# Experts on one Trainium2 core: a second pair of PSUM banks for gate and up, gathers that skip empty slots, and a first gather ahead of the gates

## The chip, the cores and the metric

The kernel runs on one core of one Trainium2 chip. The metric is the device time of one execution in microseconds (us), the median of several runs. The engines of the core are PE (TensorE: matmuls and transposes; its weight loads are listed apart as PEld), DVE (VectorE), ACT (ScalarE), POOL (GpSimd) and SP (SyncE, which only starts transfers). Matmul results land in PSUM, which has eight banks of 128 x 512 float32; all that an engine multiplies or adds lies in SBUF, and weights come from the chip's memory by DMA.

## The reference

Two transformer blocks are computed for 512 tokens of width 1024. The change is in the second block's last layer, a mixture of 32 experts in 4 groups of 8: each token takes the best group, and in it the best two experts. The final norm follows it.

```python
def hier_moe(hn, w_rg, b_rg, w_re, b_re, w_gate, w_up, w_down):
    g_prob = jax.nn.softmax((xt @ w_rg + b_rg).astype(jnp.float32), axis=-1)
    p_grp, grp = lax.top_k(g_prob, 1)
    e_logits = (xt @ w_re + b_re).astype(jnp.float32).reshape(T, N_GROUPS, EXPERTS_PER_GROUP)
    e_logits = jnp.take_along_axis(e_logits, grp[:, :, None], axis=1)[:, 0]
    p_e, e_loc = lax.top_k(jax.nn.softmax(e_logits, axis=-1), TOP_K_INNER)
    gate = p_grp * p_e / jnp.sum(p_e, -1, keepdims=True)
    expert = grp * EXPERTS_PER_GROUP + e_loc
    ...
    def run_block(args):                 # the tokens of one expert
        e, toks, gts = args
        xb = x_pad[toks]
        hid = jax.nn.silu(xb @ w_gate[e]) * (xb @ w_up[e])
        return (hid @ w_down[e]) * gts[:, None].astype(xb.dtype)
    ...                                  # added back to the tokens' rows
```

The width of an expert's hidden layer is 512. 512 tokens with two experts each are 1024 assignments.

## The kernel before

The first 1,700 us or so are the first block and the attention and projections of the second; the change doesn't touch them. What follows is the router and the experts.

**Router** (class `Router`). For each of the four blocks of 128 tokens, `block` works out the logits, the two chosen experts, and `R[token, expert]`: the token's place in the expert's queue, counted from 1, or 0 where the token isn't of that expert (L1858). `full` (L1861) finds experts with more tokens than the 64 places that each has (CAP, L1701); `gates` (L1871) makes the gate weights `Gt`.

**Slots** (L1937). The experts are taken in pairs: pair n is experts 2n and 2n+1, whose 64 places each make 128 slots on the 128 partitions. `gather(n)` (L1950) makes four 0/1 matrices OH (token by slot, L1954, DVE), multiplies them by the table `ti` of 68 columns (token number, gates and norm factors, each in two parts; L1959, four matmuls, which need the gates), reads the token number of each slot (L1961, L1964) and has POOL fetch the 128 rows of 4 KB from memory by an indirect DMA (L1966). A slot that no token holds gets row 0. The rest of the table gives the slot's scale factors (L1970 to L1975). `turned(xs)` (L1978) turns the fetched rows with two times four transposes on PE (L1985) and copies them out of PSUM (one of the two copies by ACT, one by DVE, L174 and L178).

**moe** (L1990). The loop goes over q = 0 to 7 and pr = 0, 1; n = 2q + pr. For each n:
- CT, the transposed 0/1 matrix, by DVE (L2000).
- gate into PSUM bank G and up into bank U (L2001, both of the name "f", which has two banks): 64 matmuls of 64 columns by 512 (L2008), with the weights of the two experts in the two halves of PE's columns.
- silu(G) * U into `hid` (`silu_mul`, ACT L1894, DVE L1895 and L1896), four transposes of `hid` (L2014), a copy (hT).
- down: 2 x 16 matmuls (L2024) into a bank of the name "s"; ACT and DVE take it out as yhi (L2027) and ylo (L2028).
- `turned` for n+1 and `gather` for n+2.
- After every second n (and after n = 14) the results are added to the tokens' rows: for each of 2 halves of the columns and 4 token blocks one **scatter** group, four matmuls (two after n = 14; L1934) of CT with yhi and ylo into a bank, and one DVE addition x += bank (L2045). The banks of the four blocks are "pv", "acc", "s", "s" (L2043).

PSUM's eight banks are "f" x2, "s" x2, "tp" x2 (all transposes, and gather's table), "pv" x1, "acc" x1. A name's banks are handed out in turn (`acc`, L145), and the next holder waits until the last reader of the one before is done.

**Weights** (class `Experts`, L1900). 192 pieces of 1 MB, each fetched by two transfers of 512 KB from SP's queue (one piece by POOL's) into 16 buffers in turn (L1919), in the order in which moe uses them.

**Tail** (L2048 to L2075). The last pair's scatter, the final norm's sums of squares (ACT), two `rsqrt` for two token blocks each, scaling of both halves of the columns (ACT h0, DVE h1), and eight transfers out.

`moe_rest` (L2078) handles experts with more than 64 tokens; PE and the other engines load its count `ni` and jump past it (L2086, L2087), since there are none.

The order of the instructions on an engine isn't that of the source: the program is laid out by a planner that places each instruction where it expects it to be ready. The trace shows the order that came out (scatter groups stand between the down matmuls and the next gate matmuls, for instance).

Of the kernel before, what the change touches and what calls it, by code (L numbers as in the profile page):

```python
# [11 lines left out]
F32 = mybir.dt.float32  # L12
F32R = mybir.dt.float32r
# [1923 lines left out]
class Slots:  # L1937


    def __init__(self, K, keep, xnd, Gt, R, r4, pool, mc):  # L1940
        self.K, self.xnd, self.R, self.pool, self.mc = K, xnd, R, pool, mc
        nc = K.nc
        self.ti = ti = keep.tile([P, 4, 68], F32R, name="ti")
        nc.vector.tensor_copy(ti[:, :, 0:2], mc["tok2"].rearrange("p (b c) -> p b c", b=4))
        K.split(ti[:, :, 2:34], ti[:, :, 34:66], Gt)
        K.split(ti[:, :, 66:67], ti[:, :, 67:68], r4[:, :, None])
        self.ready = [self.gather(0), self.gather(1)]

    def gather(self, n):
        K, nc, pool = self.K, self.K.nc, self.pool  # L1950
        e0 = 2 * n
        OH = pool.tile([P, 4, P], F32R, name="OH", bufs=2)
        for b in range(4):
            nc.vector.tensor_tensor(OH[:, b].rearrange("p (e s) -> p e s", e=2),  # L1954
                                    self.mc["iota64"][:, None, :].to_broadcast([P, 2, 64]),
                                    self.R[:, b, e0:e0 + 2, None].to_broadcast([P, 2, 64]), op=OP.is_equal)
        pt = K.acc("tp")
        for b in range(4):
            nc.tensor.matmul(pt[:, :68], OH[:, b], self.ti[:, b], start=b == 0, stop=b == 3)  # L1959
        tg = K.sm.tile([P, 4], F32, name="tg")  # L1960
        nc.vector.tensor_copy(tg[:, 0:1], pt[:, 0:1])  # L1961

        row = K.sm.tile([P, 1], I32, name="row")
        nc.vector.tensor_scalar(row, pt[:, 0:1], -1.0, 0.0, op0=OP.add, op1=OP.max)  # L1964
        xs = pool.tile([P, D], F32, name="xs", bufs=2)
        nc.gpsimd.indirect_dma_start(xs, None, self.xnd, bass.IndirectOffsetOnAxis(ap=row[:, 0:1], axis=0))  # L1966
        for s in range(2):
            hs = slice(64 * s, 64 * s + 64)
            e = e0 + s
            nc.vector.tensor_copy(tg[hs, 1:2], pt[hs, 2 + e:3 + e])  # L1970
            nc.vector.tensor_add(tg[hs, 1:2], tg[hs, 1:2], pt[hs, 34 + e:35 + e])
        nc.vector.tensor_copy(tg[:, 2:3], pt[:, 66:67])
        nc.vector.tensor_add(tg[:, 2:3], tg[:, 2:3], pt[:, 67:68])
# [422 lines left out]
```

## Time and profile before

| | us |
|---|---|
| median of 3 runs | 2228.69 (2226.29 to 2232.9) |
| the profiled execution, its own time | 2238.75 |
| its span, first to last instruction | 2237.0 |
| mean granted TensorE clock in it | 0.965 |
| from the first expert's gate matmul (1727.61) to the last down matmuls' begin (2214.36) | 486.75 |
| one q in the middle of it (four experts) | 62.56 |

All times of single instructions below are positions in the span of the profiled execution, which took 10.06 us more than the median of the runs. A row of a timeline gives the start, the duration, the engine, the line of the kernel, what is written and read, how many instructions stand together, and in brackets an idle time of the engine before it and what ended that.

### The profile page before, as it was taken

What the parts mean: (1) busy time and instruction counts of PE and PEld (TensorE: products, weight loads), DVE (VectorE), ACT (ScalarE), POOL (GpSimd) and SP (SyncE); (2) the same over time, 40 slices, a digit from 0 to 9 for tenths busy, and PEclk for the clock granted to TensorE, in tenths of its full rate; (3) what the DMA queues carried; (4) which work ended last, traced back from release to release, by engine and by line L of the source; (5) the groups of instructions that cost most, each with busy time, mean ns of one, the idle gap of its engine ahead of it and who ended that gap; (6) DMA issues with size and microseconds to landing.
All of it is one profiled execution on the core that took longest, in us unless ns stands there. A gap on an engine that the chain in (4) does not pass through costs nothing.

```text
span 2237.0 us, 28592 instructions
## 1 busy us (share of the span) xinstructions
PE 2086.9 (93%) x10252; PEld 1476.5 (66%) x10252; DVE 1074.4 (48%) x2554; ACT 712.5 (32%) x1507; POOL 485.6 (22%) x391
## 2 busy tenths in 40 slices
PE   7999899998999999979988999999997999999997
PEld 5777676686888888867777867777875433333332
DVE  5272226427764545475877656555445322222223
ACT  4253334433353434234532235543441110000102
POOL 2312331233133222233331121232131000000000
PEclk9899999999999999999998799999998999999999
DMA  5512332256242332133334342485257999999994
GB/s 174 162 47 67 94 97 73 67 173 230 73 138 96 98 99 95 58 112 107 101 116 108 105 162 91 156 260 167 94 187 264 403 416 413 413 415 414 413 415 182
DMA packets 203370, 411.39 MB, mean 184 GB/s; under 512 B 49192, under 2 KB 67752, under 8 KB 203096
## 3 DMA queue, kind: packets, MB, share of 16 engines
q1 hardware_dynamic: 200632, 400.08, 51.0%
q0 software_dynamic: 2592, 9.44, 1.1%
q8 instruction: 82, 1.34, 0.3%
q14 instruction: 64, 0.52, 0.1%
HBM read 371.46 MB, written 33.13 MB: 181 GB/s over the span
## 4 chain that ended last, share of the span: by engine, by line
PE 68%; DVE 12%; DMA 7%; issue 3%; ACT 3%; POOL 2%; SPq 0%; DVEq 0%; ACTq 0%; POOLq 0%
PE f L135 23%; PE f L2008 10%; PE s L2024 6%; PE acc L135 6%; PE s L135 6%; PE tp L135 2%; POOL w L128 2%; PE pv L269 1%; PE tp L261 1%; PE s L1934 1%; DMA wraw<-w2f 1%; PE pv L135 1%; ACT w L125 1%; DMA wraw<-wout 1%; PE pv L1934 1%
## 5 line engine op out<-in xcount | busy, mean ns | idle before, releaser
L128 POOL TENSOR_TENSOR w<-wraw,w 128x512 fp32r<-128x512 f32 x310 | 407.2, 1325 | 1074.1 <-ACT w L125 962.0
L125 ACT CAST w<-wraw 128x512 fp32r<-128x512 f32 (+1 forms) x446 | 261.6, 617 | 242.2 <-issue 51.7
L135 PE MATMUL f<-hhi,w 128*128 128x512 f32 (+1 forms) x832 | 281.0, 410 | 2.0 <-ACT w L125 0.7
L128 DVE TENSOR_TENSOR w<-wraw,w 128x512 fp32r<-128x512 f32 (+1 forms) x136 | 116.3, 856 | 189.6 <-ACT w L125 186.5
L2008 PE MATMUL f<-mw,xT 128*64 128x512 f32 x832 | 206.8, 594 | 0.0
L135 PE MATMUL f<-h2hi,w 128*128 128x512 f32 (+1 forms) x672 | 203.7, 384 | 0.3 <-POOL w L128 0.3
L135 PEld LDWEIGHTS f<-hhi,w 128*128 128x128 f32 x832 | 161.8, 200 | 35.1 <-issue 3.2
L135 PE MATMUL acc<-hhi,w 128*128 128x512 f32 (+1 forms) x512 | 169.3, 398 | 4.9 <-ACT w L125 1.9
L135 PE MATMUL f<-hlo,w 128*128 128x512 f32 (+1 forms) x416 | 170.0, 409 | 0.2 <-DVE hlo L187 0.2
L2008 PEld LDWEIGHTS f<-mw,xT 128*64 128x64 f32 x832 | 65.5, 137 | 124.6 <-issue 117.7
L135 PEld LDWEIGHTS f<-h2hi,w 128*128 128x128 f32 x672 | 125.2, 188 | 25.6 <-POOL w L128 0.5
L135 PE MATMUL f<-h2lo,w 128*128 128x512 f32 (+1 forms) x336 | 129.0, 384 | 0.0
L2024 PE MATMUL s<-mw,hT 128*64 128x512 f32 x416 | 121.8, 600 | 3.3 <-ACT hT L174 1.9
L135 PEld LDWEIGHTS acc<-hhi,w 128*128 128x128 f32 x512 | 96.3, 191 | 28.5 <-issue 4.3
L1966 POOL DMA_INDIRECT xs<-xnd,row x16 | 15.2, 953 | 423.3 <-DVE wraw L2000 171.0
L135 PE MATMUL acc<-hlo,w 128*128 128x512 f32 (+1 forms) x256 | 101.3, 396 | 0.0
L135 PEld LDWEIGHTS f<-hlo,w 128*128 128x128 f32 x416 | 83.1, 200 | 16.2 <-issue 1.4
L1895 DVE SCALAR_TENSOR_TENSOR hid<-hid,f 128x512 f32<-128x512 f32 x16 | 11.0, 688 | 160.3 <-ACT hid L1894 160.3
L1894 ACT ACTIVATE hid<-f,tg 128x512 f32<-128x512 f32 x16 | 11.0, 688 | 204.1 <-PE f L2008 204.1
L2024 PEld LDWEIGHTS s<-mw,hT 128*64 128x64 f32 x416 | 33.2, 136 | 59.6 <-issue 51.5
L135 PEld LDWEIGHTS f<-h2lo,w 128*128 128x128 f32 x336 | 63.1, 188 | 12.3
L2027 ACT ACTIVATE yhi<-s,tg 128x512 fp32r<-128x512 f32 x32 | 22.0, 688 | 150.8 <-PE s L2024 150.8
(743 smaller groups left out, 3991.4 us busy)
## 6 DMA issues: line engine op xcount, KB each, us to landing
mw<-wexp SPq DMA_DIRECT2D x310, 512.0 KB
w<-wexp SPq DMA_DIRECT2D x72, 512.0 KB
wraw<-wup SPq DMA_DIRECT2D x88, 256.0 KB
wraw<-w2f SPq DMA_DIRECT2D x76, 256.0 KB
wraw<-wgate SPq DMA_DIRECT2D x64, 256.0 KB
wraw<-wdown SPq DMA_DIRECT2D x44, 256.0 KB
wraw<-w1f SPq DMA_DIRECT2D x40, 256.0 KB
gated<-gt SPq DMA_DIRECT2D x28, 256.0 KB
```

What stands on the lines that cost most here:

```text
L125: nc.scalar.copy(hi[:, s], raw)
L128: eng.tensor_sub(lo[:, s], raw, hi[:, s].bitcast(F32))
L135: self.nc.tensor.matmul(out, l, r, start=start and i == 0, stop=stop and i == 2)
L261: nc.tensor.transpose(pt[:, off:off + P], Pt[s][i][:, j * P:(j + 1) * P], K.ident)
L269: one = lambda s: nc.tensor.matmul(o[64 * s:64 * s + 64, j * P:], v_of(j, s), ptS[s][:, at[j]:at[j] + n], start=start and j == 0, stop=sto ...
L1894: nc.scalar.activation(t, G, AF.Tanh, scale=half)
L1895: nc.vector.scalar_tensor_tensor(t, t, 1.0, G, op0=OP.add, op1=OP.mult)
L1934: K.nc.tensor.matmul(o, CT[:, b * P:(b + 1) * P], y[:, hs], start=start and i == 0, stop=i == len(items) - 1)
L1966: nc.gpsimd.indirect_dma_start(xs, None, self.xnd, bass.IndirectOffsetOnAxis(ap=row[:, 0:1], axis=0))
L2008: nc.tensor.matmul(o[64 * s:64 * s + 64], xT[:, kk, 64 * s:64 * s + 64], ws[s][k], start=kk == 0, stop=kk == 7)
L2024: nc.tensor.matmul(o[64 * s:64 * s + 64], hT[:, c, 64 * s:64 * s + 64], ws[s][c], start=c == 0, stop=c == 3)
L2027: nc.scalar.activation(yhi[:, hs], o, AF.Copy, scale=tg[:, 1:2])
```

## The change

- `Slots` is made early, in front of the router, with its tiles in the pool `keep`; its table is split into `tok` (2 columns) and `ti` (66 columns). Two of its row buffers are set to zero by POOL.
- `gather` becomes `rows` and `scales`. `rows(n)` makes OH, multiplies it by `tok` alone, and asks for the rows. A slot without a token gets a row number above 511, and the transfer leaves such rows out (bounds_check). `scales(n)` multiplies OH by the rest of the table in four further matmuls.
- `first()` asks for the rows of pairs 0 and 1 before the gates are computed; `router.full` comes after.
- G and U are the two "f" banks for pr = 0, and "pv" and "acc" for pr = 1.
- All scatter groups use the two "s" banks, which down uses too.
- The tail makes one `rsqrt` for all four token blocks, and scales and sends the second half of the columns first; the first half is scaled by ACT and POOL in turn.

```diff
 class Slots:
-        self.ti = ti = keep.tile([P, 4, 68], F32R, name="ti")
...
-        self.ready = [self.gather(0), self.gather(1)]
+        self.tok = keep.tile([P, 4, 2], F32R, name="tok")
+        nc.vector.tensor_copy(self.tok, mc["tok2"].rearrange("p (b c) -> p b c", b=4))
+        self.ti = keep.tile([P, 4, 66], F32R, name="ti")
+        self.xs = [keep.tile([P, D], F32, name="xs", bufs=2) for _ in range(2)]
+        for t in self.xs:
+            nc.gpsimd.memset(t, 0.0)
+    def first(self, R, Gt, r4):
+        self.R = R
+        rows = [self.rows(n) for n in range(2)]
+        K, ti = self.K, self.ti
+        K.split(ti[:, :, 0:32], ti[:, :, 32:64], Gt())
+        K.split(ti[:, :, 64:65], ti[:, :, 65:66], r4[:, :, None])
+        self.ready = [self.scales(*r) for r in rows]
     def gather(self, n):
+        return self.scales(*self.rows(n))
+    def rows(self, n):
...
         for b in range(4):
-            nc.tensor.matmul(pt[:, :68], OH[:, b], self.ti[:, b], start=b == 0, stop=b == 3)
+            nc.tensor.matmul(pt[:, :2], OH[:, b], self.tok[:, b], start=b == 0, stop=b == 3)
...
+        none = K.sm.tile([P, 1], F32, name="none")
+        nc.vector.tensor_scalar(none, pt[:, 0:1], 0.5, 2.0 * T, op0=OP.is_lt, op1=OP.mult)
+        row = K.sm.tile([P, 1], I32, name="row")
+        nc.vector.scalar_tensor_tensor(row, pt[:, 0:1], -1.0, none, op0=OP.add, op1=OP.add)
         nc.vector.tensor_copy(tg[:, 0:1], pt[:, 0:1])
-        row = K.sm.tile([P, 1], I32, name="row")
-        nc.vector.tensor_scalar(row, pt[:, 0:1], -1.0, 0.0, op0=OP.add, op1=OP.max)
-        xs = pool.tile([P, D], F32, name="xs", bufs=2)
-        nc.gpsimd.indirect_dma_start(xs, None, self.xnd, bass.IndirectOffsetOnAxis(ap=row[:, 0:1], axis=0))
+        xs = self.xs[n] if n < 2 else pool.tile([P, D], F32, name="xs", bufs=2)
+        nc.gpsimd.indirect_dma_start(xs, None, self.xnd, bass.IndirectOffsetOnAxis(ap=row[:, 0:1], axis=0),
+                                     bounds_check=T - 1, oob_is_err=False)
+        return n, OH, tg, xs
+    def scales(self, n, OH, tg, xs):
+        pt = K.acc("tp")
+        for b in range(4):
+            nc.tensor.matmul(pt[:, :66], OH[:, b], self.ti[:, b], start=b == 0, stop=b == 3)
...
 def moe(K, x, slots, weights, pool, mc, out):
-            G, U = K.acc("f"), K.acc("f")
+            G, U = (K.acc(t) for t in (("f", "f"), ("pv", "acc"))[pr])
...
-                    o = K.acc(("pv", "acc", "s", "s")[b])
+                    o = K.acc("s")
...
-    os_ = [K.acc(t) for t in ("pv", "acc", "f", "f")]
+    os_ = [K.acc(t) for t in ("f", "f", "pv", "acc")]
...
-    for p in range(2):
-        for b in (2 * p, 2 * p + 1):
-            nc.scalar.activation(j[:, h1], os_[b], AF.Square, accum_out=ss[:, b, 1:2])
-        s = ss[:, 2 * p:2 * p + 2]
-        nc.vector.tensor_add(s[:, :, 0], s[:, :, 0], s[:, :, 1])
-        r = K.rsqrt(s[:, :, 0], 1.0 / D, 1e-6, 2)
...
+    for b in range(4):
+        nc.scalar.activation(j[:, h1], os_[b], AF.Square, accum_out=ss[:, b, 1:2])
+    nc.vector.tensor_add(ss[:, :, 0], ss[:, :, 0], ss[:, :, 1])
+    r = K.rsqrt(ss[:, :, 0], 1.0 / D, 1e-6, 4)
+    for b in range(4):
+        rows = out[b * P:(b + 1) * P]
+        nc.vector.scalar_tensor_tensor(x[:, b, h1], os_[b], r[:, b:b + 1], g[:, h1], op0=OP.mult, op1=OP.mult)
+        nc.sync.dma_start(rows[:, h1], x[:, b, h1])
+        if b % 2:
+            nc.gpsimd.tensor_scalar(x[:, b, h0], x[:, b, h0], r[:, b:b + 1], None, op0=OP.mult)
+        else:
+            nc.scalar.activation(x[:, b, h0], x[:, b, h0], AF.Copy, scale=r[:, b:b + 1])
+        nc.sync.dma_start(rows[:, h0], x[:, b, h0])
...
-    upto, ni = router.full(keep)
-    Gt = router.gates(keep)
+    g = []
+    slots.first(router.R, lambda: g.append(router.gates(keep)) or g[0], r4)
+    Gt = g[0]
+    upto, ni = router.full(keep)
     RT.close()
...
-    slots = Slots(K, keep, xnd, Gt, router.R, r4, K.pool(E, "slots"), mc)
```

## Rows read from the trace of the kernel before

**Rows 1.** The page's first part: busy time, share of span, count of instructions.

```profile
PE 2086.9 (93%) x10252; PEld 1476.5 (66%) x10252; DVE 1074.4 (48%) x2554; ACT 712.5 (32%) x1507; POOL 485.6 (22%) x391
```

**Rows 2.** Windows: one q's length, five engines' busy times, clock, DMA share, GB/s.

```profile
1845.62:1908.18 62.56, 60.18 (x258) 23.46 (x260) 17.45 (x50) 5.88 (x9) 1.88 (x2) 1.00 1.03 413
```

**Rows 3.** PE's waits by releaser, 1750 to 2190: sum, count, median of one.

```profile
PE tp L2014 <- DVE hid L1896: 11.0, 13, 0.9
PE s L2024 <- DVE hT L178: 2.4, 7, 0.3
PE s L2024 <- ACT hT L174: 1.9, 7, 0.3
```

**Rows 4.** The same for SP's queue, which starts the weights' transfers.

```profile
SPq L1919 <- DMA mw<-wexp: 259.2, 272, 2.8
SPq L1919 <- PE f L2008: 3.7, 14, 0.5
```

**Rows 5.** Instruction groups by form, 1740 to 2190: busy, mean ns, idle before.

```profile
L2008 PE MATMUL f<-mw,xT 128*64 128x512 f32 x746 | 184.7, 593 | 0.0
```

**Rows 6.** Timeline of PE, pair 1: the gather's four matmuls and what follows.

```profile
1776.94 0.61 PE L1959 MATMUL tp<-ti,OH 128*128 128x68 f32 x4
1777.39 0.48 PE L1934 MATMUL pv<-yhi,wraw 128*128 128x512 f32 x1
```

**Rows 7.** Timeline of PE, pairs 6 to 8: gate, down and scatter matmuls.

```profile
1908.11 13.95 PE L2008 MATMUL f<-mw,xT 128*64 128x512 f32 x62
...
1929.99 1.07 PE L2024 MATMUL s<-w,hT 128*64 128x512 f32 x2
1930.99 0.50 PE L1934 MATMUL pv<-yhi,wraw 128*128 128x512 f32 x1
...
1958.98 0.40 PE L1934 MATMUL pv<-ylo,wraw 128*128 128x512 f32 x1
...
1960.16 0.40 PE L1934 MATMUL s<-ylo,wraw 128*128 128x512 f32 x1
1960.63 0.50 PE L1934 MATMUL pv<-yhi,wraw 128*128 128x512 f32 x1
...
1961.73 3.65 PE L2024 MATMUL s<-mw,hT 128*64 128x512 f32 x14
1965.31 0.50 PE L1934 MATMUL s<-yhi,wraw 128*128 128x512 f32 x1
...
1968.15 0.50 PE L1934 MATMUL pv<-ylo,wraw 128*128 128x512 f32 x1
```

**Rows 8.** Timeline of DVE, same stretch: two of the scatter's additions.

```profile
1959.90 0.68 DVE L2045 TENSOR_TENSOR x<-x,pv 128x512 f32<-128x512 f32 x1
...
1968.68 0.69 DVE L2045 TENSOR_TENSOR x<-x,pv 128x512 f32<-128x512 f32 x1 [1.20 <-PE pv L1934]
```

**Rows 9.** Timeline of all engines, from the first OH to the turned rows.

```profile
1714.83 0.25 DVE L1954 TENSOR_TENSOR OH<-mciota,Rexp 128x128 fp32r<-128x128 f32 x1
...
1716.64 1.89 PE L1959 MATMUL tp<-ti,OH 128*128 128x68 f32 x8 [2.38 <-DVE ti L187]
...
1718.22 1.13 POOL L1966 DMA_INDIRECT xs<-xnd,row  x1 [9.71 <-DVE tg L1970]
...
1725.67 1.94 PE L1985 MATMUL tp<-ident,xs 128*128 128x128 f32 x8 [7.14 <-DMA xs<-xnd,row]
```

**Rows 10.** Line view: PE's jump past moe_rest (shortest, median, longest ns; when).

```profile
L2087 PEldq COMPARE_BRANCH  x1: 6279/6279/6279, 1717.3 to 1717.3; - x1
```

**Rows 11.** DMA, 1640 to end: the gathers' count and median us to landing.

```profile
xs<-xnd,row POOLq DMA_INDIRECT x16, 8.1
```

**Rows 12.** Groups of POOL, whole span: the nearest memset to the added ones.

```profile
L1254 POOL MEMSET BD<- 128x1024 f32 x2 | 1.9, 960 | 9.0 <-PE tp L234 9.0
```

**Rows 13.** Timeline of the end: the last scaling and the last transfer out.

```profile
2230.89 1.41 DVE L2074 SCALAR_TENSOR_TENSOR x<-f,ny,xT 128x512 f32<-128x512 f32 x2
...
2233.12 0.39 SPq L2075 DMA_DIRECT2D out<-x  x1
```

More of the change, by code (lines that the diff above doesn't have):

```diff
@@ L1937, with __init__ @@
 class Slots:
-    def __init__(self, K, keep, xnd, Gt, R, r4, pool, mc):
-        self.K, self.xnd, self.R, self.pool, self.mc = K, xnd, R, pool, mc
+    def __init__(self, K, keep, xnd, mc):
+        self.K, self.xnd, self.pool, self.mc = K, xnd, keep, mc
         nc = K.nc
-        self.ti = ti = keep.tile([P, 4, 68], F32R, name="ti")
-        nc.vector.tensor_copy(ti[:, :, 0:2], mc["tok2"].rearrange("p (b c) -> p b c", b=4))
-        K.split(ti[:, :, 2:34], ti[:, :, 34:66], Gt)
-        K.split(ti[:, :, 66:67], ti[:, :, 67:68], r4[:, :, None])
-        self.ready = [self.gather(0), self.gather(1)]
+        self.tok = keep.tile([P, 4, 2], F32R, name="tok")
[11 more added lines that the diff above has]
+        self.ready = [self.scales(*r) for r in rows]
     def gather(self, n):
+        return self.scales(*self.rows(n))
+    def rows(self, n):
         K, nc, pool = self.K, self.K.nc, self.pool
@@ L1969, in gather @@
             e = e0 + s
[L1970 to L1973, printed above, removed]
+            nc.vector.tensor_copy(tg[hs, 1:2], pt[hs, e:1 + e])
+            nc.vector.tensor_add(tg[hs, 1:2], tg[hs, 1:2], pt[hs, 32 + e:33 + e])
+        nc.vector.tensor_copy(tg[:, 2:3], pt[:, 64:65])
+        nc.vector.tensor_add(tg[:, 2:3], tg[:, 2:3], pt[:, 65:66])
         nc.vector.scalar_tensor_tensor(tg[:, 3:4], tg[:, 2:3], 0.5, tg[:, 2:3], op0=OP.mult, op1=OP.mult)
@@ L2063, in moe @@
         scatter(K, os_[b], parts, b, h1, False)
-    for p in range(2):
-        for b in (2 * p, 2 * p + 1):
-            nc.scalar.activation(j[:, h1], os_[b], AF.Square, accum_out=ss[:, b, 1:2])
-        s = ss[:, 2 * p:2 * p + 2]
-        nc.vector.tensor_add(s[:, :, 0], s[:, :, 0], s[:, :, 1])
-        r = K.rsqrt(s[:, :, 0], 1.0 / D, 1e-6, 2)
-        for i, b in enumerate((2 * p, 2 * p + 1)):
-            rows = out[b * P:(b + 1) * P]
-            nc.scalar.activation(x[:, b, h0], x[:, b, h0], AF.Copy, scale=r[:, i:i + 1])
-            nc.sync.dma_start(rows[:, h0], x[:, b, h0])
-            nc.vector.scalar_tensor_tensor(x[:, b, h1], os_[b], r[:, i:i + 1], g[:, h1], op0=OP.mult, op1=OP.mult)
-            nc.sync.dma_start(rows[:, h1], x[:, b, h1])
+    for b in range(4):
[11 more added lines that the diff above has]
+        nc.sync.dma_start(rows[:, h0], x[:, b, h0])
 def moe_rest(K, x, r4, gT, Gt, R, upto, ni, hnd):
@@ L2281, in block2 @@
     weights = Experts(K, {"keep": keep, "mm": mp})
+    slots = Slots(K, keep, xnd, mc)
     ss = rt.tile([P, 4, 2], F32, name="ssr")
```

8 lines of the change are left out of this document (5 added, 3 removed).

## The prediction, made before the change was run

> **What bounds the kernel now.** I read the page's busy times first: PE is busy for 93% of the span, no other engine for half of it [rows 1]. Busy time is an average, so the second view is the stage that the change touches, in windows cut at the same step of each q. All q in the middle take 62.56 us, with PE busy for 60.18 at full clock (1.00), DVE for 23.46, and DMA at a share of 1.03 and 413 GB/s [rows 2]. Two things are full at once there, so the third view asks which waits for the other. PE's list of waits has 15.3 us in 440 us, all of them for the turn from hid to down (11.0 for hid, 2.4 + 1.9 for hT) [rows 3]; no weight transfer is in the list, and the gate matmuls have no idle time before them at all [rows 5]. SP's queue waits 259.2 us for earlier transfers and 3.7 us for a buffer that PE still holds [rows 4]. So the transfers run at their own pace, just ahead of PE, and PE's order of instructions sets the end. A saving of DMA time reaches the end only if PE becomes faster than the transfers; a matmul that is added to PE's order reaches it at once, unless it falls into one of the 15.3 us.
>
> The fourth view, PE's timeline, shows what PE's time holds beyond work. In an unbroken run, 62 gate matmuls take 13.95 us, of which the last one's own length (0.59, the mean of rows 5) is tail: 13.36 / 61 = 0.219 us a step, 3.50 for 16. Where two of 16 stand apart, they hold PE 1.00 us (1929.99 to 1930.99), and the other 14 take 3.58 (1961.73 to 1965.31): 4.58 against 3.50, so a break between 64-column and 128-column work costs 1.08 us [rows 7]. The down and gate matmuls around a scatter have some five such breaks in each q.
>
> **Part 1, the split of the gather.** Pairs 0 and 1 are asked for in the start. For the other 14, four matmuls become eight: four of 2 columns and four of 66, and PE loads OH twice. The nearest row is the old four of 68 columns: the next instruction starts 0.45 us after the first of them (1776.94 to 1777.39) [rows 6]. I take the same for the four new ones, though they have 2 columns, since they need the same weight loads: 14 x 0.45 = **+6.3 us**. Bounds: 0 if they fall into the 0.9 us wait for hid [rows 3], which is at the same place of the pair; 14 x 1.08 = +15 if each set breaks a run of 64-column matmuls anew [rows 7]. The two instructions for the row number become two longer ones plus the copy: one more on DVE, 0.15 us where DVE idles for more than half of a q [rows 2]: 0.
>
> The Trainium skill (Perfetto Trace Analysis, section Optimizing Tensor Performance, Matmuls) says that larger matmuls are more efficient than smaller ones. It speaks against this part; taken as if columns alone counted, the four would cost 2/68 of 0.45 and the term would be +0.2 instead of +6.3. No row has a matmul of 2 columns.
>
> **Part 2, the banks of gate and up.** A second pair lets the gate matmuls of n+1 start before silu of n has read its banks. In the trace they never wait for that: no such line in PE's waits, 0.0 idle before them [rows 3, 5]. They come too late for it: the transposes of the rows for n+1 stand behind those of hid in the two "tp" banks, and these are after silu. Gain 0. Bounds: 0 to the whole of the 15.3 us (a rival, below).
>
> **Part 3, scatter on two banks instead of four.** A bank comes free when the addition has read it. Without a crowd this is 1.22 us after the group's last matmul begins (1968.15 to 1968.68 + 0.69); where DVE has other work in its queue, the addition begins at 1959.90 after a matmul of 1958.98, and the bank's next matmul stands at 1960.63: 1.65 us [rows 7, 8]. A matmul steps on by 0.236 us (1958.98 to 1960.16 in five steps), so a group of four needs 0.94 us, and one bank turns in 3 x 0.236 + 1.22 = 1.93 to 2.36 us. Two banks in turn give a group each 0.96 to 1.18 us against PE's 0.94: +0.02 to +0.24 for each of 8 groups, +0.2 to +1.9 in a q. In the middle 1.05, by 7.5 (seven whole scatters and n = 14's half one): **+7.9 us**. Since down holds one of the two banks for its 16 matmuls and its way out, a group that comes then has one bank alone and loses about 1.0 more (1.93 - 0.94). Upper bound (1.9 + 1.0) x 7.5 = +22. Lower bound: the planner puts 64-column work between the groups at no cost, and one break in each q goes, since the order is laid anew: 7 x -1.08 = -7.6. Nothing excludes it.
>
> **Part 4, rows of empty slots.** 16 gathers of 128 rows of 4 KB are 8.39 MB; at most 1024 of 2048 slots hold a token, so 4.2 MB or more go: 10.1 us of transfers at 413 GB/s [rows 2]. PE waits for none of them: **0**, bounds 0 to -10.1.
>
> **Part 5, the start.** PE waits 2.38 us for ti, which needs the gates [rows 9]. In the change the first matmuls need only OH. Four OH of 0.25 us from 1714.83 on end at 1715.8, against 1716.64: -0.8; the gates' own small DVE instructions no longer stand between them: -0.3 more by my estimate. The request, now at 1718.22, moves by that, and the rows land as long after it as now (8.1 us in the median of the 16) [rows 11]: **-1.1 us**. What is late next is PE itself: its jump past moe_rest takes 6.28 us from 1717.3 to 1723.6 [rows 10], 2.1 us before the rows' landing releases it at 1725.67 [rows 9]. In the change the count ni is made after the gates and PE has eight more small matmuls ahead of the jump; each us that it starts later eats what is left of the 2.1. Bounds -2.0 to +1.0. Moved past on queues: POOL's gathers are ahead of nothing else there; SP goes on with weights. The two memsets take 0.96 us each on POOL by the nearest row [rows 12]; they stand ahead of the router, beside POOL's small work there: 0, at most +1.9 if the router's chain stood behind them.
>
> **Part 6, the tail.** One rsqrt for four blocks saves a chain of a dozen small DVE instructions, but the first transfer out waits for all four squares instead of two. Now the last scaling is two instructions of 0.7 us from 2230.89, and the last transfer is issued at 2233.12 [rows 13]. Then eight issues of about 0.4 us each, one after the other on SP, start when the first scaling is done, about 2230.0, and end near 2233.4: **+0.3**, bounds -1 to +1.5.
>
> **The sum.** 6.3 + 0 + 7.9 + 0 - 1.1 + 0.3 = +13.4 us. The profiled execution took 2238.75 of its own, 1.75 more than its span, and 10.06 more than the median of the runs; nothing in the stage's rows makes the difference depend on that, so I add it to the median: 2228.69 + 13.4 = 2242.
>
> **Rivals.** (a) *Absorbed.* The new matmuls land in the wait for hid, and scatter's groups are spread between down and gate matmuls, as some are now (the banks' group of 1965.31 follows 14 down matmuls) [rows 3, 7]. For it: 0.9 us of wait against 0.45 of work in each pair. Against it: in the trace the gather's matmuls stand after hid's transposes, not before. Then only start and tail count: 2228.69 - 1.1 + 0.3 = 2228, with scatter's lower values up to 2233.
>
> (b) *Faster: the second bank pair fills the turn.* If the planner brings the next pair's rows and gate matmuls ahead of hid's transposes, the 15.3 us of rows 3 go, and the start's 1.1; the split still costs 6.3: 2228.69 - 15.3 - 1.1 + 6.3 + 0.3 = 2219, and 2212 if a break goes too. The transfers, which run just ahead of PE, can follow only because part 4 frees 10.1 us. The deciding point is whether the first transposes of rows n+1 come to stand before those of hid n on PE. For it: the source now allows gate n+1 beside silu n. Against it: one half of these transposes needs a "tp" bank that hid's transposes still hold.
>
> The Trainium skill (same page and section) states that independent matmul groups should rotate through different PSUM banks so that one's evacuation overlaps the next group's matmuls. For gate and up this is rival (b); for scatter, which goes from four banks to two, it speaks for part 3. In this trace the gate matmuls wait for no bank, so I side with the rows.
>
> (c) *The first gather isn't earlier:* PE's jump holds it, part 5 gives 0, and the time is 2243; within the forecast's own range.
>
> **How the numbers follow.** A measurement of this kernel can tell about 0.3%, 6.7 us, from no change: faster is under 2222.0, slower over 2235.4. The forecast (2236 to 2262, with (c) in it) has 0.46, (a) 0.24, (b) 0.30. The predicted time is the forecast's, 2242. The upper end of its own range is the sum with scatter at its upper bound (+14) and half of part 1's (+4 to +6): 2262. The range reaches down into (b): 2213 to 2262, which leaves out some 0.1 at the bottom and 0.05 at the top.
>
> **What would show it.** In the changed kernel's windows a q should take about 62.56 + 2 x 0.45 + 1.05 = 64.5 us. PE's waits should have a new line for scatter's matmuls released by DVE's addition; the lines for hid and hT should stay at about 15 us. SP's waits for transfers should shrink in favour of waits for PE. The first gather's issue should stand near 1717.1. What would make it wrong: rows' transposes ahead of hid's, no wait on the "s" banks, or the four 2-column matmuls at far below 0.45 us.

## The result, and the profile after

The changed kernel takes 2254.11 us (median of 4 runs, 2246.66 to 2257.66) against 2228.24 for the kernel before in the same comparison; the ratio of the runs is 1.009, with a 95% interval of 1.0062 to 1.0119. By the ratio it is slower by 20 us (14 to 27 by the interval); the two medians are 25.9 us apart. The forecast was 2242 in a range of 2213 to 2262, slower.

The profiled execution took 2252.2 us (span 2250.4), only 13.4 us of span more than that of before. The two differ in what comes ahead of the experts too: the last of the four places in the experts' queues (DVE's instruction of L1858, called R below) stands at 1711.01 us in this trace and at 1714.30 in that of before, although nothing ahead of it changed but two memsets and a small copy. Over all traces of this case R lies between 1698.8 and 1714.3. What the change touches is the stretch from R to the end: 522.7 us before, 539.4 after, **+16.7 us**. This stretch is what the traces are compared by from here on; it lies within the 14 to 27 us of the runs, near their lower end.

The page's first part, columns as in [rows 1]:

```profile
PE 2092.5 (93%) x10316; PEld 1481.3 (66%) x10316; DVE 1075.7 (48%) x2557; ACT 711.1 (32%) x1505; POOL 492.8 (22%) x395
```

64 matmuls more, 16 times four, and 5.6 us of busy time: the rest of the loss is not work. One q in the windows, columns as in [rows 2]. The five engines there are PE, PEld, DVE, ACT and POOL, in this order: the 23.46 us that the prediction gives to DVE are those of the weight loads, and DVE's are 17.45. Nothing hangs on it, since DVE idles all the more.

```profile
1969.55:2032.99 63.44, 59.81 (x265) 24.10 (x264) 18.46 (x52) 5.89 (x9) 1.98 (x2) 1.00 1.03 409
```

A q takes 63.44 us instead of 62.56, while PE is busy for less, 59.81 instead of 60.18, with eight matmuls more. PE's waits in the stage (1750 to 2200) say what it is doing, columns as in [rows 3], where the third number is the longest single wait and not the median:

```profile
PE tp L2040 <- DVE hid L1896: 12.0, 14, 0.9
PE s L1934 <- DVE x L2071: 7.6, 9, 1.1
PE s L1934 <- DVE ylo L2054: 2.8, 7, 1.6
PE s L2050 <- DVE hT L178: 2.4, 7, 0.3
PE s L2050 <- ACT hT L174: 1.9, 7, 0.3
```

The turn from hid to down is as it was. The second and the third line are new, 10.4 us: scatter waits for its two banks, for the addition that reads one, or for ylo, which reads what down left in it. Both read the bank in PSUM itself (`x<-x,s` and `ylo<-s`), so the first section's words that all that an engine adds lies in SBUF are wrong for DVE here. SP's queue waits four times as long as in [rows 4] for buffers that PE holds, so PE is further behind the transfers than before:

```profile
SPq L1919 <- PE f L2034: 15.0, 14, 2.5
```

PE's timeline around one scatter shows the new waits and, above them, the split gather:

```profile
1956.46 0.58 PE L1974 MATMUL tp<-tok,OH 128*128 128x2 f32 x4
1956.98 3.65 PE L2050 MATMUL s<-mw,hT 128*64 128x512 f32 x14
1960.56 0.63 PE L1992 MATMUL tp<-ti,OH 128*128 128x66 f32 x4
1961.12 1.07 PE L2050 MATMUL s<-mw,hT 128*64 128x512 f32 x2
...
1962.39 0.47 PE L1934 MATMUL s<-yhi,wraw 128*128 128x512 f32 x1 [0.19 <-DVE ylo L2054]
...
1963.16 0.39 PE L1934 MATMUL s<-ylo,wraw 128*128 128x512 f32 x1
1964.64 0.50 PE L1934 MATMUL s<-yhi,wraw 128*128 128x512 f32 x1 [1.09 <-DVE x L2071]
...
2189.68 0.50 PE L1934 MATMUL s<-yhi,wraw 128*128 128x512 f32 x1 [1.62 <-DVE ylo L2054]
...
2191.19 0.50 PE L1934 MATMUL s<-yhi,wraw 128*128 128x512 f32 x1 [0.78 <-DVE x L2071]
```

The group that ends with the matmul of 1963.16 should be added at once. DVE's timeline shows what stands ahead of the addition in DVE's queue: ylo and the gather's small instructions, one after the other (ten rows between the first and the last are left out):

```profile
1961.23 0.15 DVE L1996 COPY tg<-tp 64x1 f32<-64x1 f32 x1 [3.72 <-PE tp L1992]
...
1961.50 0.74 DVE L2054 SCALAR_TENSOR_TENSOR ylo<-s,tg,yhi 128x512 fp32r<-128x512 f32 x1
...
1963.84 0.15 DVE L2001 TENSOR_SCALAR tg<-tg 128x1 f32<-128x1 f32 x1
1963.91 0.68 DVE L2071 TENSOR_TENSOR x<-x,s 128x512 f32<-128x512 f32 x1
```

The start, all engines, as [rows 9]; the row after it is the line view of PE's jump, as [rows 10]:

```profile
1711.01 0.19 DVE L1858 SCALAR_TENSOR_TENSOR Rexp<-pv,Aexp 128x32 f32<-128x32 f32 x1 [0.76 <-PE pv L1856]
...
1712.70 1.09 POOL L1982 DMA_INDIRECT xs<-xnd,row  x1 [7.48 <-DVE sp L1886]
...
1720.66 1.73 PE L2011 MATMUL tp<-ident,xs 128*128 128x128 f32 x7 [4.93 <-PEq L2114]
1723.25 0.47 PE L2011 MATMUL tp<-ident,xs 128*128 128x128 f32 x1 [0.86 <-issue]
1723.65 5.39 PE L2034 MATMUL f<-w,xT 128*64 128x512 f32 x12
```

```profile
L2114 PEldq COMPARE_BRANCH  x1: 5634/5634/5634, 1714.6 to 1714.6; - x1
```

The rows are asked for 1.69 us after R (before: 3.92) and land at 1719.56, 8.55 us after R (before: 11.23, and 10.56 in the second trace of that kernel, e1 below). But PE turns them when it is back from its jump (1714.6 + 5.63 = 1720.2), not when they land: the releaser of its idle time is the jump's line, where in [rows 9] it was the gather.

The end, SP's first and last transfer out, as in [rows 13]:

```profile
2242.09 0.34 SPq L2102 DMA_DIRECT2D out<-x  x1
...
2245.96 0.60 SPq L2102 DMA_DIRECT2D out<-x  x1
```

PE's last matmul ends at 2235.55 (before: 2224.66); the first transfer out follows after 6.54 us (before: at 2228.81, after 4.15), the last after 10.41 (before: 8.46).

### The profile page after: what moved, and what is told of

It reads as the page before. It is cut to its first block, busy times and chain, and to the rows that moved or that the text cites. A ratio compares the mean times of both kernels' runs of the same rounds, so it can differ in the third digit from the quotient of the medians.

```text
span 2250.4 us, 28758 instructions
## 1 busy us (share of the span) xinstructions
PE 2092.5 (93%) x10316; PEld 1481.3 (66%) x10316; DVE 1075.7 (48%) x2557; ACT 711.1 (32%) x1505; POOL 492.8 (22%) x395
## 3 DMA queue, kind: packets, MB, share of 16 engines
q0 software_dynamic: 2592, 5.25, 0.6%
## 5 line engine op out<-in xcount | busy, mean ns | idle before, releaser
L2034 PE MATMUL f<-mw,xT 128*64 128x512 f32 x416 | 101.9, 594 | 0.0
L2034 PEld LDWEIGHTS f<-mw,xT 128*64 128x64 f32 x416 | 32.2, 137 | 62.4 <-issue 60.3
L996 DVE SCALAR_TENSOR_TENSOR cv<-f,cw,cv 128x511 f32<-128x511 f32 x41 | 30.7, 750 | 67.5 <-ACT cv L995 67.5
L2034 PE MATMUL acc<-mw,xT 128*64 128x512 f32 x224 | 62.3, 593 | 0.0
```

The lines of the kernel that those rows point to most:

```text
L996: nc.vector.scalar_tensor_tensor(t[:, 1:], u[:, :T - 1], c[:, 1:2], t[:, 1:], op0=OP.mult, op1=OP.add)
L2034: nc.tensor.matmul(o[64 * s:64 * s + 64], xT[:, kk, 64 * s:64 * s + 64], ws[s][k], start=kk == 0, stop=kk == 7)
```

## The experiments

**How the traces are summed up.** For each kernel the table has the ratio to the kernel before with its 95% interval; from the trace the span and R, and span minus R; one q in the middle (from pair 8's first gate matmul to pair 10's) and PE's busy time in it, from the windows. The last three columns are counted over PE's matmuls in the trace, from the first gate matmul to the last scatter matmul: the time with no matmul in flight (idle), the rest of that stretch (busy), and the breaks, which are the places where PE's order goes from 64-column matmuls (gate, down) to others and back, each way counted as half.

| kernel | ratio (95%) | span - R = us | q | PE busy in q | idle | busy | breaks |
|---|---|---|---|---|---|---|---|
| before, first profile | | 2237.0 - 1714.3 = 522.7 | 62.56 | 60.18 | 20.3 | 476.8 | 72.5 |
| e1 before again | 1.0005 (0.9975 to 1.0035) | 2233.9 - 1712.3 = 521.5 | 62.56 | 60.17 | 20.3 | 476.3 | 72.5 |
| changed | 1.009 (1.0062 to 1.0119) | 2250.4 - 1711.0 = 539.4 | 63.44 | 59.81 | 31.2 | 480.7 | 70.5 |
| e2 changed, all old banks | 1.0012 (0.9984 to 1.0039) | 2236.8 - 1711.9 = 524.9 | 61.85 | 59.50 | 20.1 | 478.1 | 70.5 |
| e3 before, scatter on s | 1.001 (0.9982 to 1.0038) | 2239.8 - 1709.9 = 530.0 | 62.78 | 59.00 | 32.2 | 472.5 | 68.5 |
| e4 before, split gather | 0.9996 (0.9968 to 1.0023) | 2227.8 - 1701.7 = 526.1 | 61.83 | 59.48 | 20.0 | 477.6 | 69.5 |
| e5 before, two pairs | 0.9996 (0.9976 to 1.0016) | 2220.8 - 1701.6 = 519.2 | 61.46 | 58.66 | 24.3 | 469.7 | 67.5 |
| e6 changed, old scatter banks | 1.002 (0.9995 to 1.0045) | 2230.8 - 1703.3 = 527.5 | 62.48 | 59.68 | 24.6 | 476.9 | 68.5 |
| e7 changed, one pair | 1.007 (1.0041 to 1.0099) | 2237.6 - 1698.8 = 538.8 | 63.44 | 59.81 | 31.2 | 480.3 | 70.5 |
| e8 before, new tail | 1.0005 (0.9984 to 1.0025) | 2223.6 - 1700.3 = 523.3 | 62.56 | | 20.3 | 475.8 | 72.5 |
| e9 changed, no jump | 1.0065 (1.0039 to 1.009) | 2239.5 - 1703.5 = 536.0 | 63.45 | | 31.4 | 480.2 | 70.5 |
| e10 changed, scatter on pv, acc | 1.007 (1.0043 to 1.0096) | 2247.1 - 1704.4 = 542.7 | 64.14 | 60.96 | 26.6 | 489.0 | 79.5 |
| e11 e2 with all rows fetched | 1.0013 (0.999 to 1.0036) | 2235.2 - 1709.9 = 525.3 | 61.85 | 59.50 | 20.1 | 477.5 | 70.5 |
| e12 the parts that cost nothing | 0.9968 (0.9945 to 0.9991) | 2217.9 - 1700.5 = 517.3 | 61.47 | 58.67 | 23.9 | 468.2 | 66.5 |

A single run scatters by some 10 us either way (the kernel before ran from 2217.66 to 2244.02), so runs alone hardly tell effects under 5 us apart; the stretch from R on repeats within 1.2 us. (The 20 us of the changed kernel are from four runs; e7, 0.6 us shorter in that stretch, is slower by 0.7% in nine runs, 16 us.)

**e1, the control.** No edit.

> The kernel before, run once more as a control, with a second profile. The first profiled execution of it took 10.06 us more than the median of its runs, and a comparison of its trace with that of the changed kernel shows +13.4 us where the medians differ by 25.9. Theory: what comes ahead of the router varies from execution to execution by some 10 us, and the experts stage does not; then from the last block's places in the queues (1714.30 in the first trace) to the end this trace again has 522.7 us, within 1 us, and the ratio is 1.000 within 0.3%. Rival: the experts stage itself varies; then this stretch differs by several us from 522.7.

521.5 instead of 522.7, and 1.10 of the 1.15 us lie ahead of the second pair's gate matmuls, at the start and in the first pair; each later q is the same within 0.02 us:

```profile
1964.06:2026.62 62.56, 60.17 (x257) 23.47 (x256) 17.44 (x50) 5.88 (x9) 1.87 (x2) 1.00 1.03 414
```

So the experts stage repeats and what comes ahead of the router doesn't. The +13.4 us between the spans was too small by what R happened to be.

**e2, the banks undone in the changed kernel.**

```diff
-            G, U = (K.acc(t) for t in (("f", "f"), ("pv", "acc"))[pr])
+            G, U = K.acc("f"), K.acc("f")
...
-                    o = K.acc("s")
+                    o = K.acc(("pv", "acc", "s", "s")[b])
...
-    os_ = [K.acc(t) for t in ("f", "f", "pv", "acc")]
+    os_ = [K.acc(t) for t in ("pv", "acc", "f", "f")]
```

> The changed kernel with the banks of before: gate and up always in f, scatter in pv, acc, s, s, the tail's banks as before. Everything else stays (split gather, skipped rows, first gather ahead of the gates, tail). Theory of the forecast: scatter on two banks is the largest term; PE's waits for DVE's additions (7.6 us) and for ylo (2.8 us) in the changed kernel go, and the time falls from 2254 by 8 to 10 us, to about 2244 to 2246, which still is some 16 us above before. Rival: the banks carry all of it, because the planner's order goes back with them; then the time is about 2228 + 6 = 2234 or below. Rival: they carry nothing; 2254.

524.9: 14.5 us of the 16.7 go with the banks, about the first rival's figure and not the 8 to 10 of my theory. The rival's reason didn't come, though: the order didn't go back to that of before (70.5 breaks, as in the changed kernel, and not 72.5). The waits for the addition and for ylo are gone. What is left, +2.2 to +3.4 against the two profiles of before, is about the tail's share alone (e8). And a q is at 61.85, below the 62.56 of before, with eight matmuls more:

```profile
1969.17:2031.02 61.85, 59.50 (x265) 24.33 (x265) 18.02 (x52) 5.88 (x9) 1.98 (x2) 1.00 1.03 409
```

**e3, scatter on the two s banks alone.** The edit of the second pair of lines above, turned round, in the kernel before.

> The kernel before with one edit: all scatter groups use the two s banks, gate and up stay on f. Theory of the forecast: +7.9 us (bounds -7.6 to +22), about 2236, with PE waiting for DVE's additions by the s banks. Rival: the second pair of banks for gate and up has its share in the loss through the order; then this alone costs under 3 us.

530.0, +7.3 and +8.4 against the two profiles of before: the forecast's +7.9. But it is a sum of two that partly cancel: PE's idle time grows by 11.9 us, and the order that the planner lays has four breaks less, with 3.8 to 4.3 us less of busy time. PE's waits have the two lines of the changed kernel, in a kernel that has nothing else of the change:

```profile
PE s L1934 <- DVE x L2045: 6.8, 7, 1.0
PE s L1934 <- DVE ylo L2028: 4.2, 7, 1.6
```

**e4, the split of the gather alone.**

```diff
-            nc.tensor.matmul(pt[:, :68], OH[:, b], self.ti[:, b], start=b == 0, stop=b == 3)
+            nc.tensor.matmul(pt[:, :2], OH[:, b], self.ti[:, b, 0:2], start=b == 0, stop=b == 3)
...
+        pt = K.acc("tp")
+        for b in range(4):
+            nc.tensor.matmul(pt[:, 2:68], OH[:, b], self.ti[:, b, 2:68], start=b == 0, stop=b == 3)
```

> The kernel before with one edit: the gather's four matmuls of 68 columns become four of 2 and four of 66 columns, the latter in a further tp bank; rows of empty slots are still fetched and the first gathers stay where they were. Theory of the forecast: 14 x 0.45 = +6.3 us, about 2234.5, with a q of 63.4 to 63.5 us instead of 62.56. Rival (columns alone count): +0.2 us. Rival (each new set breaks a run of 64-column matmuls): up to +15 us, about 2243.

526.1, +3.4 and +4.5 against before. None of the three theories has it as it came out. A q became shorter, 61.83 us, because the new order has nine breaks in a q instead of ten. The first four pairs take 6.4 us more, with 13.5 breaks instead of 11.5, but ten of scatter's matmuls (2.4 us at 0.236 each) have moved into them from later. Idle and busy time of the whole stage together are 497.6 us, only 0.5 to 1.0 more than before. The larger part of the loss is the start: the first gate matmul stands at R + 16.07 instead of R + 13.31 (R + 12.64 in e1). There PE does the first two pairs' added matmuls ahead of its jump, which begins at R + 5.3 instead of R + 3.0 and holds it for 6.12 us; the rows wait for PE, not PE for the rows, and once more for 1.97 us ahead of the eighth transpose:

```profile
1713.69 1.73 PE L1988 MATMUL tp<-ident,xs 128*128 128x128 f32 x7 [6.20 <-PEq L2090]
...
1717.39 0.47 PE L1988 MATMUL tp<-ident,xs 128*128 128x128 f32 x1 [1.97 <-issue]
```

and the window of one q:

```profile
1962.37:2024.20 61.83, 59.48 (x266) 24.33 (x265) 17.67 (x50) 5.88 (x9) 1.88 (x2) 1.00 1.03 413
```

**e5, two pairs of banks for gate and up alone.** The first edit of e2 turned round, in the kernel before.

> The kernel before with one edit: gate and up take the banks pv and acc for pr = 1; scatter stays on pv, acc, s, s. So far, from the last places in the queues (R) to the end: before 522.7 and 521.5 us, changed kernel 539.4, changed kernel with all old banks 524.9, before with scatter on s 530.0. Theory of the forecast (part 2): nothing, since the gate matmuls never waited for a bank; 522 within 2 us, PE's waits for hid and hT as before. Rival (b): the turn is filled, PE's waits for hid (11.0 us) shrink, 510 or so. Rival: the second pair costs by itself, about the 6.7 us that scatter on s leaves of the 14.5 between old and new banks.

519.2, 2.3 to 3.5 us faster than the two profiles of before, just outside the 2 us that my theory gave. The turn isn't filled: PE still waits 11.4 us for hid, and 4.6 us are new, scatter waiting for pv until silu has read it. What is gained is order: 67.5 breaks instead of 72.5, a q at 61.46.

```profile
PE tp L2014 <- DVE hid L1896: 11.4, 14, 0.9
PE pv L1934 <- DVE hid L1895: 4.6, 6, 1.1
```

**e6 and e7, one of the two bank edits undone in the changed kernel.** e6 has scatter on pv, acc, s, s; e7 has gate and up on f; the lines are those of e2.

> The changed kernel with scatter on pv, acc, s, s again, gate and up on the two pairs. If the terms add: scatter's 7.8 us go, 539.4 - 7.8 = 531.6 from R to the end. If scatter on two banks is all of the banks' loss in the changed kernel, and gate and up cost nothing: about 525. If scatter on pv and acc now collides with gate and up on the same banks: above 531.6, with PE waits for pv or acc.

> The changed kernel with gate and up always on f, scatter on the two s banks. If gate and up's pair costs nothing: 539.4 from R to the end, with the same waits for DVE's additions (6.6 us) and ylo (2.8 us). If the terms add to e2's 524.9: 524.9 + 7.8 = 532.7, and the pair costs 6.7.

e6 has 527.5 and e7 538.8. Scatter on two banks costs 539.4 - 527.5 = 11.9 us beside the two pairs, 538.8 - 524.9 = 13.9 beside the one; the two pairs cost 0.6 us where scatter is on s, and 2.6 where it is on four banks (with 4.9 us of waits for pv, much as in e5). Some of this is the start, which neither edit touches: PE's jump happened to take 4.32 us in e6 and 4.88 in e2, against 5.63 in the changed kernel and 5.80 in e7, and the first gate matmul stands at R + 11.43, 12.17, 12.64 and 12.79. Counted from that matmul on, scatter costs 10.7 us beside the two pairs and 13.2 beside the one, and the two pairs cost 0.8 and 3.4. So scatter is the loss, and the terms don't add: the 7.8 of e3 are not what it costs here. The difference is the order: in e3 the waits come with four breaks less, in the changed kernel the split has taken the cheaper order already (e2 and e7 both have 70.5 breaks), and the waits stand bare, 31.2 - 20.1 = 11.1 us of idle time, and 2.1 more busy.

**e8, the new tail alone.** The tail of the changed kernel in the kernel before, with os_ on pv, acc, f, f.

> The kernel before with the changed kernel's tail (one rsqrt for four blocks, second half first, POOL scaling every other first half), its banks as before. Theory of the forecast: +0.3 us (bounds -1 to +1.5) from the last pair's first down matmul to the end, 26.1 before. The traces of the changed kernel (28.7) and of the one with old banks (28.3) speak for a rival, +2.2: the first transfer out waits for all four blocks. Then this kernel has 28.3 there and nothing else moves.

From the last pair's first down matmul to the end 28.37 us, 26.1 before: +2.3, the rival. The fourth square ends, a chain of thirteen small DVE instructions follows, and the first transfer out stands 1.8 us behind its last. The rows are the end of the fourth square, the end of the chain and SP's first transfer:

```profile
2211.03 0.19 ACT L2065 ACTIVATION_READ_ACCUMULATOR xs<-f 128x1 f32 x1
...
2213.65 0.16 DVE L209 SCALAR_TENSOR_TENSOR ny<-nt,ny 128x4 f32<-128x4 f32 x1
...
2215.59 0.34 SPq L2076 DMA_DIRECT2D out<-x  x1
```

**e9, without the jump.** The call of `moe_rest` is left out of the changed kernel.

> The changed kernel without the call of moe_rest, so without its load of the count and its jump on every engine (what handles experts with more than 64 tokens is left out; no expert has more here). In the changed kernel the first rows land 8.55 us after R (before: 11.23), but the first gate matmul stands at R + 12.64, as in the second profile of before, because PE comes out of its jump only at R + 9.2 and then waits 0.86 us once more. Theory: the jump ate the gain of the earlier gather; without it PE turns the rows at R + 8.6 and gate begins at about R + 11.0, 1.6 us earlier. Rival: the rows' own way (landing, transposes, copy) sets the start; then it stays within 0.5 us of R + 12.64. Nothing else should move by over 2 us from R to the end beyond that gain.

The first gate matmul stands at R + 9.89, 2.75 us earlier (I had 1.6), and from R to the end it is 536.0, 3.4 us less. PE's idle time is now ended by the rows' landing:

```profile
1703.51 0.19 DVE L1858 SCALAR_TENSOR_TENSOR Rexp<-pv,Aexp 128x32 f32<-128x32 f32 x1 [0.76 <-PE pv L1856]
...
1711.46 1.94 PE L2011 MATMUL tp<-ident,xs 128*128 128x128 f32 x8 [3.23 <-DMA xs<-xnd,row]
1713.40 3.02 PE L2034 MATMUL f<-w,xT 128*64 128x512 f32 x10
```

The jump ate the whole gain of the earlier gather. Its price was more than the hold itself: with it PE also stood still for 0.86 us between the seventh and the eighth transpose and gate came later still. The other kernels with this start say the same. In four of them (e2, e7, e10, e11) and in the changed kernel the rows have landed when the jump ends, at R + 8.3 (e2) to R + 9.4 (e11), and gate begins 3.5 to 3.8 us behind that end. In e6 the jump ends at R + 7.8, ahead of the landing at R + 8.5, and gate stands at R + 11.43, the earliest of those with a jump.

**e10, two banks that are not shared with down.**

```diff
-            G, U = (K.acc(t) for t in (("f", "f"), ("pv", "acc"))[pr])
+            G, U = K.acc("f"), K.acc("f")
...
-                    o = K.acc("s")
+                    o = K.acc(("pv", "acc")[b % 2])
```

> The changed kernel with gate and up on f and all scatter groups on the two banks pv and acc, which nothing else uses then; down keeps s to itself. Two banks as in the changed kernel (538.8 us from R to the end with gate and up on f), but not shared with down. Theory (the forecast's part 3 in two terms): turning two banks costs 0.2 to 1.9 us in a q, sharing one of them with down about 1.0 more; without sharing, the wait for ylo (2.8 us) goes and some of the waits for additions stay, about 530 to 534. Rival: the number of banks is all, 538 again. Rival: sharing is all, 525 as with the old banks (524.9).

542.7, more than with the shared banks and more than any of the three expectations. The waits behave as the theory had it: no wait for ylo any more, 4.9 us for additions, and the idle time falls from e7's 31.2 to 26.6 us; by this, sharing with down would be some 4.6 of the 11.1 us and the turning of two banks the other 6.5, as far as a kernel in another order can tell. For the planner lays another order, with 79.5 breaks instead of 70.5, and the busy time grows by 8.7 us. One q has 60.96 us of PE's busy time for the same 264 matmuls:

```profile
1966.48:2030.62 64.14, 60.96 (x265) 24.21 (x264) 18.21 (x52) 5.88 (x9) 1.98 (x2) 1.00 1.03 408
```

What sharing costs under an unchanged order wasn't tried; the order can't be held while banks change.

**e11, rows of empty slots fetched again.** In e2's kernel:

```diff
-        nc.vector.tensor_scalar(none, pt[:, 0:1], 0.5, 2.0 * T, op0=OP.is_lt, op1=OP.mult)
...
-        nc.vector.scalar_tensor_tensor(row, pt[:, 0:1], -1.0, none, op0=OP.add, op1=OP.add)
+        nc.vector.tensor_scalar(row, pt[:, 0:1], -1.0, 0.0, op0=OP.add, op1=OP.max)
...
-                                     bounds_check=T - 1, oob_is_err=False)
```

> The changed kernel with the old banks (e2, 524.9 us from R to the end) in which the gathers fetch row 0 for empty slots again, so that 4.2 MB more are moved in the stage. Theory (part 4): 0, a q at 61.85 us as in e2, since PE waits for no transfer. Rival: the transfers set the pace; 4.2 MB at 413 GB/s are 10.1 us over the stage, 0.9 to 1.4 us in a q.

525.3 against 524.9, and a q of 61.85 in both. Leaving the rows out is worth nothing here.

**e12, the parts that cost nothing, together.** Two pairs of banks, scatter on four, the old tail; for the first two pairs the small table first and moe_rest ahead of their scale factors, one table for all other pairs:

```diff
-        for b in range(4):
-            nc.tensor.matmul(pt[:, :66], OH[:, b], self.ti[:, b], start=b == 0, stop=b == 3)
+        n, OH, tg, xs, pt = self.fetch(n, *self.table(n, self.ti, 68))
...
-                    o = K.acc("s")
+                    o = K.acc(("pv", "acc", "s", "s")[b])
...
+    slots.first(router.R)
+    upto, ni = router.full(keep)
+    Gt = router.gates(keep)
...
     moe_rest(K, x, r4, gT, Gt, router.R, upto, ni, hnd)
+    slots.second(Gt, r4)
```

> The parts that cost nothing, together: gate and up on two pairs, scatter on pv, acc, s, s, the old tail, one table matmul of 68 columns for all pairs but the first two, rows of empty slots left out, the first two pairs' rows asked for ahead of the gates, and the jump past moe_rest ahead of the first two pairs' scale factors, so that PE's jump runs beside the gather. Base: e5 with 519.2 us from R to the end and its first gate matmul at R + 12.9. Theory: the start gains 1.5 to 2 us, 517 to 518 from R to the end, some 0.2% below before, which the runs can just not tell from no change. Rival: the planner's order changes with the start and takes it back, 520 to 523.

517.3 from R to the end, 4.2 to 5.4 us less than before, and a ratio of 0.9968 with an interval of 0.9945 to 0.9991: about 0.3% faster than before by the runs and 0.2% by the trace, and faster than the changed kernel. The total is what I expected, the reason is not. The start gained nothing (R + 12.93): the rows have landed at R + 5.86 and PE is back from its jump at R + 6.0, but it does the scale factors' matmuls first, and the transposes then wait for the tp banks that DVE still has to read (the first of them begins 0.10 us after DVE's last read of its bank, and the fifth waits for DVE by name):

```profile
1707.03 1.89 PE L1966 MATMUL tp<-ti,OH 128*128 128x68 f32 x8 [5.33 <-PEq L2125]
1709.91 1.08 PE L2023 MATMUL tp<-ident,xs 128*128 128x128 f32 x4 [0.99 <-PE tp L1966]
...
1711.39 0.87 PE L2023 MATMUL tp<-ident,xs 128*128 128x128 f32 x3 [0.40 <-DVE tg L2011]
```

The gain is in PE's busy time, 8.1 us less than e1's with 66.5 breaks instead of 72.5, against 3.6 us more of idle time.

## Why the prediction was right, and where its steps were not

**The bound** was right. PE's order sets the end: no transfer appears among PE's waits in the changed kernel, and moving 4.2 MB less or more changes nothing (e11, part 4: 0 forecast, 0.4 us measured, less than the 1.2 by which two profiles of one kernel differ).

**Part 3, scatter** (forecast +7.9, bounds -7.6 to +22), is the loss, as forecast, and was mis-sized: 11.9 to 13.9 us in the changed kernel, or 10.7 to 13.2 from the first gate matmul on (e6, e7). The waits are those that the step named, the bank's way through DVE's queue, and sharing with down. A whole scatter was sized nearly right, with some luck: in a q of the middle it waits 1.28 us (1.09 for the addition and 0.19 for ylo) against the 1.05 of the step. A q is 0.96 us longer than e6's, and in e7 1.59 longer than in e2. But it waits at two places, where PE comes back to a bank whose reader is ylo or stands behind ylo and the gather's small instructions (the rows of DVE above), and not a little at each of eight groups; the middle between an empty and a crowded queue only happened to come near. Two things were wrong in the sum. It counted n = 14's scatter as half of a whole one: with two matmuls in a group PE needs 0.47 us for it, while the banks turn as slowly as before, so the half scatter waits 2.40 us, nearly as much as two whole ones; the waits of 1.62 and 0.78 us at 2189.68 and 2191.19 are these. And it had no term for PE's busy time, which is 2.1 us more than e2's in e7, at the same number of breaks. The lower bound's one break less in each q came true (nine instead of ten), but by the split, not by the banks.

**Part 1, the split** (forecast +6.3): the price of the matmuls was right. The four of 2 columns hold PE for 0.52 us (1956.46 to 1956.98), the four of 66 for 0.56 (1960.56 to 1961.12); over a q of nine breaks eight matmuls more make PE's busy time 59.50 instead of 58.66 (e2 against e5), 0.42 for each four against the 0.45 of the step. The Trainium skill's rule that larger matmuls are more efficient (Perfetto Trace Analysis, section Optimizing Tensor Performance, Matmuls) agrees with this: four matmuls of 2 columns cost nearly as much as four of 66. The +0.2 us that columns alone would give, which the prediction set beside the rule, is not what the rule says, and was no candidate. The upper bound of +15, a new break for each set, was none either. In the kernel before, the gather's four matmuls already stood on both sides of 14 down matmuls, as the rows show, and the two sets of the changed kernel took the same two places (1956.46 and 1960.56 above):

```profile
1953.18 0.39 PE L1959 MATMUL tp<-ti,OH 128*128 128x68 f32 x2
1953.50 3.65 PE L2024 MATMUL s<-mw,hT 128*64 128x512 f32 x14
1957.08 0.41 PE L1959 MATMUL tp<-ti,OH 128*128 128x68 f32 x2
```

But the sum of the step failed: I let the order of the rest stand, and it was laid anew, with one break less in each q. With the old banks the split came to 1.1 to 1.6 us over the stage instead of 6.3 (idle and busy time together 498.2 in e2, 496.6 and 497.1 before). That is also why a q, forecast at 64.5 us, took 63.44.

**The price of a break** (1.08 us in the forecast) holds, as an average: no run changes the breaks alone, but kernels with the same number of matmuls can be compared. Their busy times differ by (476.3 - 468.2) / 6 = 1.35 us a break (e1, e12), (489.0 - 478.1) / 9 = 1.21 (e10, e2), (489.0 - 480.3) / 9 = 0.97 (e10, e7) and (476.3 - 472.5) / 4 = 0.95 (e1, e3). One or two breaks are too few to tell, since the busy time of one and the same order differs by up to 1.0 us between traces (before, e1, e8).

**Part 2, gate and up** (forecast 0): 0.6 us in the changed kernel, 0.8 from the first gate matmul on (e7). The reason given holds: PE waits for hid as before, and the rows' transposes still stand behind those of hid (1954.17 behind 1953.68 in the q shown). Rival (b) didn't come. The Trainium skill's rule on rotating banks (same page and section) was borne out for scatter, where it spoke against the change; for gate and up, where it spoke for it, e5 shows a gain of 2.3 to 3.5 us that comes with new waits on pv and fewer breaks, not from evacuation beside matmuls.

**Part 5, the start** (forecast -1.1, bounds -2.0 to +1.0): -0.67 against the first profile, 0.00 against the second (both kernels at R + 12.64). Rival (c) came true: the gather lands 2.0 to 2.7 us earlier, and the jump, which the step named as the next in line, holds PE. That the step put the gain at -1.1 all the same was too much for a cover of 2.1 us that it saw shrinking; e9 shows what lay behind the jump.

**Part 6, the tail** (forecast +0.3, upper bound +1.5): +2.3 to +2.6 (e8, and the changed kernel's 28.68 us against 26.11). The step failed twice: the first transfer out stands 6.54 us behind PE's last matmul and not 5.3 (2230.0 less 2224.66), since the chain of thirteen starts only after the fourth square, and SP's last four issues are 0.6 to 0.7 us apart, where the step had 0.4 for each. Why SP is slower there wasn't tried.

**The sum** of the changed kernel against e1, 539.4 - 521.5 = 17.9 us: idle +10.9, busy +4.4 between the first gate matmul and the last scatter, tail +2.6, start 0. The busy part is 56 matmuls more at 0.42 for four, 5.9, less two breaks at 0.95 to 1.35, 1.9 to 2.7: 3.2 to 4.0 of the 4.4. The rest isn't settled. It may be the steps after a wait, which are longer (0.47 to 0.50 instead of 0.40): e7 has 2.1 us more of busy time than e2 at the same number of matmuls and breaks, but no run takes the waits away in the same order. The forecast's +13.4 was short by scatter's size, the tail and a start that gained nothing, and too high by the split. That these errors partly cancel is luck: scatter, the tail and the start together are some 5 to 9 us above their terms, the split some 5 below its own.

## What to carry to other kernels

Before a group of matmuls gets fewer banks, work out the banks' turn with the longest queue that stands ahead of the reader in the trace, not with the reader alone, and do it for the smallest group, since the short groups waited most here. Where an engine's order is laid by a planner, any edit in the stage may change the order elsewhere in it: count switches between kinds of matmul (here 0.95 to 1.35 us for one there and back) before and after, and judge an edit only by a run of the whole. An earlier request is worth nothing while the engine that uses its data is held by something else, so look for what else that engine does until then.

## What the runs showed of the hardware

- A matmul of 2 columns took nearly as long as one of 66: four held PE for 0.52 and 0.56 us until the next matmul began.
- A jump over a skipped block held PE for 3.81 (e12) to 6.63 us (e1) in the 13 traces that have it, 6.28 and 6.63 in two traces of the same kernel, and the other engines for 0.04 to 0.07 us. The Trainium skill (Runtime: NRT & Kernel Launch, section Instruction fetch mechanics) states that a taken branch out of the prefetched code waits for a fetch. The traces agree in that PE stood still for microseconds behind the branch; no run here shows the fetch itself, or why the other engines' jumps were short.
- Gathers that leave rows out moved fewer bytes (5.25 MB on POOL's queue instead of 9.44) in as many packets (2592), and landed in 7.4 us in the median instead of the 8.1 of [rows 11]; e11, which fetches all rows in the changed kernel with the old banks, is back at 9.44 MB and 8.1 us. The DMA view of the changed kernel, from 1640 on:

```profile
q0 software_dynamic: 2592, 5.25, 2.4%
...
xs<-xnd,row POOLq DMA_INDIRECT x16, 7.4
```
